# Feed-forward parts of a two-block model on one core: down products in four groups instead of three, and fixed places for split weights

## The chip, the cores and the metric

One NeuronCore of a Trainium2 chip runs one program. The metric is the device time of an execution in microseconds (us); less is better. Engines: TensorE (PE: matmuls, PEld: weight loads), VectorE (DVE), ScalarE (ACT), GpSimd (POOL), and SyncE (SP), whose queue issues the DMAs.

## The reference, cut to what matters

The model is two layers of a first block (feed-forward, mixer, feed-forward) and one second block (mixer, feed-forward). Five feed-forward parts have this form, on 528 tokens (512 and 16 meta tokens) or 512, with D_MODEL 1024 and D_FF 2816:

```python
def swiglu(x, w_gu, w_down):
    gate, up = jnp.split(x @ w_gu, 2, axis=-1)
    return (jax.nn.silu(gate) * up) @ w_down

h = h + 0.5 * swiglu(rms_norm(h, ffn_norm[l]), ffn_w_gu[l], ffn_w_down[l])
```

## The kernel before, in words

All activations are transposed: 8 tiles h[0..7] of 128 features by 528 (or 512) tokens stay on the chip. Every fp32 product is made of three matmuls in fp32r: weights and activations are split into a rounded part (hi) and the rest (lo), and PE adds hi·hi, hi·lo and lo·hi. Weights come from memory as *chunks* of 128 x 1024 fp32 or less into four raw tiles (RAW = 4, line 285); ACT copies the hi part (`hi`, line 364, tile whi) and DVE or POOL subtracts for the lo part (`lo`, line 367, tile wlo). A pair whi/wlo lies in one of five places (H = 5, line 284), taken in turn: chunk i goes to place i mod 5, and may be split only when chunk i-5 has been read.

A feed-forward part (`ffn`, line 559) has 22 tiles of 128 hidden features. In the five parts, called a0, b0, a1, b1 and c in order of time, gate and up of a plain tile are `gu(j)` (line 681): two chunks. All tiles of a0 are plain. In the other four only tiles 0 to 5 are; tiles 6 to 21 use a seven-product scheme: the gate and up chunk of a tile are added and subtracted in quarters on DVE, which gives four *parts* of weights (parts 0 to 2 with 1024 columns, part 3 with 512), and seven *products* (`product`, line 608) of 12 matmuls of 264 or 256 columns each. Tiles b11, B21, B22, T1 to T4 are the matching sums of activations. After the seventh product the hidden tile is split to gh and gl.

The down product of a group of hidden tiles is one chunk per output tile m (`d{group}.{m}`), accumulated over the group's tiles k in `down_steps` (line 728; one Item per k, three matmuls per column segment), then added to h[m] by DVE. THIRDS (line 29) makes three groups of 8, 7 and 7 tiles. The downs of groups 0 and 1 are interleaved by `weave` (line 267) with the products of the next group's tiles; those of group 2 come last, through `down` (line 705), without products beside them, and each finished h[m] goes to `nxt(m)`: `prep` (line 536) makes xh, xl and the sum of squares for the next stage, `prep_2` (line 1632) does so before the second block, `store` (line 2062) issues a DMA in part c.

The order of work around these stages is written out by `run` (line 329). The splitting steps of all chunks stand in one list in order of first use, and only its head can be issued. `between(cost)`, called after the matmuls of an Item and before its evacuation, issues as many steps as the cost has earned (0.9 per step, at most three saved up), while `allowed()` (line 425) holds for the head. Steps of a chunk that an Item needs are issued just before it at the latest. For Items marked `seven` (products and woven downs) the order of instructions on each engine is the order in which the code issues them (`InOrder`, line 239); chunks of such Items have their lo part on DVE, other chunks on DVE or, mostly, on POOL:

```python
e = nc.vector if i in sevens or i % 3 == 0 and c.split(".")[0] not in BUSY else nc.gpsimd
```

Of the kernel before, what the change touches and what calls it, by code (L numbers as in the profile page):

```python
# [8 lines left out]
F32 = mybir.dt.float32  # L9
# [17 lines left out]
NEG = -1e30  # L27
F_MIN = 1e-20
THIRDS = ((0, 8), (8, 15), (15, 22))
LEVELS = (64, 32, 16, 8, 4, 2)  # L30
TOPK = 128
TAKEN = -3e38
# [10 lines left out]
def chunk_table():  # L43

    table = {}

    def add(name, nk, m, make):
        table[name] = (len(table), nk, m, make)

    def cols(key, l, idx, r0=0, r1=None):  # L50
        return lambda a: _ktile(a[key][l][r0:r1][:, idx])

    def ffn(tag, l, gate, up, down):

        def gu(j):
            add(f"{tag}g{j}", KT, 128, cols(gate[0], l, np.arange(128) + gate[1] + 128 * j))
            add(f"{tag}u{j}", KT, 128, cols(up[0], l, np.arange(128) + up[1] + 128 * j))
        for j in range(NJ):
            gu(j)
        for t, (j0, j1) in enumerate(THIRDS):  # L60
            for m in range(KT):
                add(f"{tag}d{t}.{m}", j1 - j0, 128, cols(down, l, np.arange(128) + 128 * m, 128 * j0, 128 * j1))

    r = np.arange(128)
    for l in range(DEPTH):
        ffn(f"a{l}", l, ("ffn1_w_gu", 0), ("ffn1_w_gu", D_FF), "ffn1_w_down")
        for m in range(2):
            add(f"ckv{l}.{m}", KT, 128, cols("w_in", l, 384 + 128 * m + r))
        rot = np.arange(32)
        swap = np.concatenate([rot[16:], rot[:16]])  # L70
        add(f"kpe{l}", KT, 128, cols("w_in", l, 640 + np.concatenate([rot, rot, rot, swap])))
        for m in range(3):
            add(f"cq{l}.{m}", KT, 128, cols("w_in", l, 128 * m + r))
        for j in range(HG_HEADS):
            for i, n in enumerate("qfig"):
                add(f"h{n}{l}.{j}", KT, 128, cols("w_in", l, 672 + 512 * i + 128 * j + r))
        for m in range(KT):
            add(f"ga{l}.{m}", KT, 128, cols("w_in", l, 2720 + 128 * m + r))
            add(f"gb{l}.{m}", KT, 128, cols("w_in", l, 3744 + 128 * m + r))

        def v_cols(l=l):
            idx = (np.arange(MLA_HEADS)[:, None] * 128 + 64 + np.arange(64)[None]).reshape(-1)
            return cols("w_ukv", l, idx)
        add(f"v{l}", 2, 512, v_cols())

        def qk(j, l=l):
            q1 = np.concatenate([np.arange(64), 64 + rot, 64 + swap])
            parts = [cols("w_uq", l, (2 * j + i) * 96 + q1) for i in range(2)]
            k1 = np.concatenate([(2 * j + i) * 128 + np.arange(64) for i in range(2)])
            parts.append(cols("w_ukv", l, k1))  # L90
            return lambda a: np.concatenate([p(a) for p in parts], axis=1)
        for j in range(4):
            add(f"qk{l}.{j}", 8, 128, qk(j))

        def proj(m, l=l):
            pa, pb = cols("w_proj_attn", l, 128 * m + r), cols("w_proj_rec", l, 128 * m + r)
            return lambda a: np.concatenate([pa(a), pb(a)], axis=1)
        for m in range(KT):
            add(f"pj{l}.{m}", 8, 128, proj(m))
        for m in range(KT):  # L100
            add(f"wo{l}.{m}", KT, 128, cols("w_out", l, 128 * m + r))
        ffn(f"b{l}", l, ("ffn2_w_gu", 0), ("ffn2_w_gu", D_FF), "ffn2_w_down")

    def one(name, idx, m=128):
        add(name, KT, m, cols("w_in_2", 0, idx))
    r64 = np.arange(64)
    one("kk2", np.concatenate([1408 + r64, 1024 + r64]))
    for m in range(2):
        one(f"qi2.{m}", 1152 + 128 * m + r)
    one("vw2", np.concatenate([1088 + r64, 1472 + np.arange(4)]), 68)  # L110
    for m in range(4):
        one(f"u2.{m}", 128 * m + r)
    for m in range(4):
        one(f"q2.{m}", 512 + 128 * m + r)
    for m in range(KT):
        one(f"ga2.{m}", 1476 + 128 * m + r)
        one(f"gb2.{m}", 2500 + 128 * m + r)

    def two(key0, i0, key1, i1):
        p0, p1 = cols(key0, 0, i0), cols(key1, 0, i1)  # L120
        return lambda a: np.concatenate([p0(a), p1(a)], axis=1)
    for m in range(2):
        add(f"glu2.{m}", 8, 128, two("w_glu_2", 256 * m + r, "w_glu_2", 256 * m + 128 + r))
    for m in range(KT):
        add(f"pj2.{m}", 8, 128, two("w_proj_ssm_2", 128 * m + r, "w_proj_attn_2", 128 * m + r))
    for m in range(KT):
        add(f"wo2.{m}", KT, 128, cols("w_out_2", 0, 128 * m + r))
    ffn("c", 0, ("w_ffn_gate_2", 0), ("w_ffn_up_2", 0), "w_ffn_down_2")
    return table

# [73 lines left out]
class Scalar:  # L204


    def __init__(self, tc, e):
        self.tc, self.e, self.last = tc, e, None
# [27 lines left out]
        self.cost, self.fn, self.chunks, self.seven = cost, fn, tuple(chunks), seven  # L236


class InOrder:


# [40 lines left out]
class Kernel:  # L282
# [46 lines left out]
    def run(self):  # L329
# [12 lines left out]
        def load():  # L342
            nonlocal n_dma
            idx, nk, m, _ = CHUNKS[loads[n_dma]]
            t = self.wp.tile([128, 1024], F32, tag=f"raw{n_dma % self.RAW}", name=f"raw_{n_dma}")
            nc.sync.dma_start(t[:, :nk * m], self.ins["w"][idx, :, :nk * m])
            raws[loads[n_dma]] = t
            n_dma += 1

        def drop(c):  # L350
            raws.pop(c)
            gone[load_at[c]] = True
            while n_dma < len(loads) and (n_dma < self.RAW or gone[n_dma - self.RAW]):
                load()

        def hi_lo(i):
            if i not in made:
                made[i] = [self.wp.tile([128, 1024], F32R, tag=f"{x}{i % self.H}", name=f"w{x}_{i}") for x in ("hi", "lo")]
                n = 1024 if not isinstance(order[i], str) else CHUNKS[order[i]][1] * CHUNKS[order[i]][2]
                nk = 8 if not isinstance(order[i], str) else CHUNKS[order[i]][1]  # L360
                self.split_of[order[i]] = [t[:, :n].rearrange("p (k m) -> p k m", k=nk) for t in made[i]]
            return made[i]

        def hi(i, a, b, src):
            self.sc.activation(hi_lo(i)[0][:, a:b], src, AF.Copy)

        def lo(i, a, b, src, e=nc.vector):
            h, l = hi_lo(i)
            e.tensor_tensor(l[:, a:b], src, h[:, a:b].bitcast(F32), op=OP.subtract)

        def plus(out, a, b):
            nc.vector.tensor_tensor(out, a, b, op=OP.add)
# [42 lines left out]
        for it in self.prog:  # L415
            if it.seven:
                sevens.update(range(at, at + len(it.chunks)))
            at += len(it.chunks)
        queue = []
        for i in range(len(order)):  # L420
            queue += [x if isinstance(x, tuple) else (i, x) for x in steps_of(i)]
# [3 lines left out]
        def allowed():  # L425
            if n_step == len(queue):
                return False
            i = queue[n_step][0]
            return i < self.H or done[i - self.H]

        def step():
            nonlocal n_step
# [14 lines left out]

        self.between = between
        self.read = lambda c: done.__setitem__(index[c], True)
        load()  # L450
        self.setup(load)
        self.warm()
# [106 lines left out]
    def ffn(self, tag, n, st, alpha, nxt, gname=None, l=0):  # L559
# [167 lines left out]

        def down_steps(t, m):

            j0, j1 = THIRDS[t]  # L730
            nk = j1 - j0
            at = {}
            name = f"{tag}d{t}.{m}"

            def fn(k):
                if k == 0:
                    at["ps"] = self.accum(n)
                ps, cols = at["ps"]
                x = {k: g[j0 + k][0]}, {k: g[j0 + k][1]}
                self.mm3(ps, self.split_of[name], x, k, k, cols, k == 0, k == nk - 1)  # L740
                if k == nk - 1:
                    self.read(name)
                self.between(0.73)
                if k == nk - 1:
                    for q, (a, b) in zip(ps, cols):
                        hv = self.h[m][:, a:b]
                        nc.vector.scalar_tensor_tensor(hv, q, alpha, hv, op0=OP.mult, op1=OP.add)
                    if m == KT - 1:
                        for j in range(j0, j1):
                            self.free(*g.pop(j))  # L750
            return [Item(0.73, lambda k=k: fn(k), [name] if k == 0 else (), True) for k in range(nk)]

        c = 0.22 * 3
# [12 lines left out]
        if PLAIN_J < NJ:  # L766
            for j in range(PLAIN_J):
                add_gu(j)
            for j in range(PLAIN_J, THIRDS[0][1]):
                self.prog += products(j)  # L770
            for t in (0, 1):
                p = [x for j in range(*THIRDS[t + 1]) for x in products(j)]
                self.prog += p[:4] + weave(p[4:-4], [x for m in range(KT) for x in down_steps(t, m)]) + p[-4:]
            add_down(2)
            return
        for j in range(0, 9):
            add_gu(j)
# [1306 lines left out]
```

## Time and profile before

| | |
|---|---|
| median of 3 runs | 3183.62 us (3178.26 to 3184.14) |
| profiled execution, its own time | 3182.51 us |
| span of its trace | 3180.7 us |
| PE busy | 3118.5 us, 98% |
| DVE busy | 2072.9 us, 65% |
| ACT busy | 1377.7 us, 43% |
| POOL busy | 852.9 us, 27% |

The span runs from the first to the last instruction; the execution's own time is 1.8 us longer. Matmuls are pipelined: a matmul is shown busy for longer than the next one waits, so busy time says less than the spacing of starts. "Idle before" is time in which an engine had nothing to run, with the engine and tile that ended it. A row of a view by stretches gives the stretch, its length, the busy time of PE, PEld, DVE, ACT and POOL (or of one engine) with the number of instructions in brackets, the granted TensorE clock as a share of 2.4 GHz, the DMA engines' busy share and GB/s.

### The profile page before, as it was taken

What the parts mean: (1) busy time and instruction counts of PE and PEld (TensorE: products, weight loads), DVE (VectorE), ACT (ScalarE), POOL (GpSimd) and SP (SyncE); (2) the same over time, 40 slices, a digit from 0 to 9 for tenths busy, and PEclk for the clock granted to TensorE, in tenths of its full rate; (3) what the DMA queues carried; (4) which work ended last, traced back from release to release, by engine and by line L of the source; (5) the groups of instructions that cost most, each with busy time, mean ns of one, the idle gap of its engine ahead of it and who ended that gap; (6) DMA issues with size and microseconds to landing.
All of it is one profiled execution on the core that took longest, in us unless ns stands there. A gap on an engine that the chain in (4) does not pass through costs nothing. (4 is left out here: it accounts for less than half of the span.)

```text
span 3180.7 us, 52625 instructions
## 1 busy us (share of the span) xinstructions
PE 3118.5 (98%) x21530; PEld 2872.4 (90%) x21530; DVE 2072.9 (65%) x3552; ACT 1377.7 (43%) x2355; POOL 852.9 (27%) x493
## 2 busy tenths in 40 slices
PE   9999999999999999999999999999999999999999
PEld 9999999899999999999998888888998777888888
DVE  7664466763676666866666674577667587577674
ACT  5322345544344434444444553444346435444442
POOL 3553235543220002100034453330003543230001
PEclk9999999999999999999999999999999999999999
DMA  6333331111222233223332112222334432222332
GB/s 199 123 99 108 94 94 56 44 58 61 93 80 93 88 99 113 67 94 97 94 109 74 41 47 74 86 93 74 105 107 152 124 101 73 67 93 73 99 103 91
DMA packets 106530, 289.61 MB, mean 91 GB/s; under 512 B 23088, under 2 KB 32304, under 8 KB 106288
## 3 DMA queue, kind: packets, MB, share of 16 engines
q1 hardware_dynamic: 106288, 286.24, 28.5%
q8 instruction: 169, 2.77, 0.4%
q14 instruction: 73, 0.60, 0.1%
HBM read 272.96 MB, written 13.24 MB: 90 GB/s over the span
## 5 line engine op out<-in xcount | busy, mean ns | idle before, releaser
L249 POOL TENSOR_TENSOR wlo<-raw,whi 128x1024 fp32r<-128x1024 f32 (+1 forms) x217 | 541.2, 2496 | 1965.2 <-ACT whi L249 1668.3
L249 ACT ACTIVATE whi<-raw 128x1024 fp32r<-128x1024 f32 (+2 forms) x632 | 537.9, 866 | 817.2 <-PE bank L249 417.3
L249 PE MATMUL bank<-xh,whi 128*128 128x264 f32 (+1 forms) x2504 | 811.8, 325 | 4.8 <-DVE t L249 4.3
L249 PE MATMUL bank<-xl,whi 128*128 128x264 f32 (+1 forms) x2504 | 811.3, 324 | 5.0 <-DVE xl L249 4.9
L249 PE MATMUL bank<-xh,wlo 128*128 128x264 f32 (+1 forms) x2504 | 804.9, 322 | 1.3 <-POOL wlo L249 1.3
L249 PEld LDWEIGHTS bank<-xl,whi 128*128 128x128 f32 x2504 | 476.1, 190 | 34.9 <-DVE xl L249 6.8
L249 PEld LDWEIGHTS bank<-xh,whi 128*128 128x128 f32 x2504 | 475.2, 190 | 35.4 <-issue 4.7
L249 PEld LDWEIGHTS bank<-xh,wlo 128*128 128x128 f32 x2504 | 475.6, 190 | 27.1 <-issue 1.7
L249 PE MATMUL bank<-gh,wlo 128*128 128x264 f32 (+1 forms) x1408 | 440.6, 313 | 12.1 <-DVE wlo L249 12.1
L249 DVE TENSOR_TENSOR wlo<-raw,whi 128x1024 fp32r<-128x1024 f32 (+2 forms) x351 | 368.5, 1052 | 123.0 <-ACT whi L249 120.2
L249 PE MATMUL bank<-gh,whi 128*128 128x264 f32 (+1 forms) x1408 | 439.7, 312 | 0.0
L249 PE MATMUL bank<-gl,whi 128*128 128x264 f32 (+1 forms) x1408 | 439.5, 312 | 0.0
L249 PEld LDWEIGHTS bank<-gh,wlo 128*128 128x128 f32 x1408 | 265.1, 188 | 30.2 <-DVE wlo L249 14.6
L249 PEld LDWEIGHTS bank<-gh,whi 128*128 128x128 f32 x1408 | 265.2, 188 | 8.4 <-issue 0.4
L249 PEld LDWEIGHTS bank<-gl,whi 128*128 128x128 f32 x1408 | 265.2, 188 | 8.3
L249 ACT ACTIVATE p<-p,nm 128x144 f32<-128x144 f32 (+8 forms) x104 | 57.0, 548 | 224.5 <-DVE nm L249 217.0
L249 PE MATMUL bank<-T2h,whi 128*128 128x264 f32 (+1 forms) x512 | 146.5, 286 | 3.8 <-DVE c L249 3.5
L249 DVE SCALAR_TENSOR_TENSOR h<-bank,h 128x264 f32<-128x264 f32 (+1 forms) x192 | 88.7, 493 | 92.2 <-PE bank L249 91.2
L249 PE MATMUL bank<-T2h,wlo 128*128 128x264 f32 (+1 forms) x512 | 145.8, 285 | 1.8 <-DVE wlo L249 1.8
L249 PE MATMUL bank<-B21h,whi 128*128 128x264 f32 (+1 forms) x512 | 145.5, 284 | 0.9 <-ACT zu L249 0.9
L249 PE MATMUL bank<-B21h,wlo 128*128 128x264 f32 (+1 forms) x512 | 145.3, 284 | 0.0
L249 PE MATMUL bank<-B21l,whi 128*128 128x264 f32 (+1 forms) x512 | 145.0, 283 | 0.0
(373 smaller groups left out, 6641.9 us busy)
## 6 DMA issues: line engine op xcount, KB each, us to landing
raw<-in_w_dram SPq DMA_DIRECT2D x423, 512.0 KB, 3.5
raw<-in_w_dram SPq DMA_DIRECT2D x80, 448.0 KB, 3.3
h<-in_x_dram SPq DMA_DIRECT2D x8, 264.0 KB, 6.9
s_t<-zero SPq DMA_DIRECT2D x8, 256.0 KB, 3.5
s_wo<-cm SPq DMA_DIRECT2D x16, 128.0 KB, 3.2
s_win<-cm SPq DMA_DIRECT2D x8, 256.0 KB, 2.0
s<-s_win SPq DMA_DIRECT2D x8, 256.0 KB, 4.2
s<-s_wo SPq DMA_DIRECT2D x8, 256.0 KB, 4.1
```

The source lines that it names most:

```text
L249: i = f(*args, **kw)
```

## The change

The four parts with seven-product tiles get GROUPS of 6, 6, 5 and 5 tiles; a0 keeps THIRDS. The downs of groups 0, 1 and 2 are woven with the products of groups 1, 2 and 3; in the first weave no product leads (before, 14 products of tiles 6 and 7 and four more stood ahead of it). The downs of group 3 are Items of the `seven` kind too, and call `nxt`. The places: within such a phase, part r has the place r of the five (counted from the one after the last plain chunk), downs alternate between place 4 ("even") and the second half of place 3 plus a small tile `rest` ("odd"), and a step waits for the last user of its own place only. The list of steps stays one list.

```diff
+GROUPS = ((0, 6), (6, 12), (12, 17), (17, 22))
...
+class Pieces:
+    def __getitem__(self, at):
+        p, k, m = at
+        return self.a[p, k, m] if k < self.n else self.b[p, k - self.n, m]
...
         def hi_lo(i):
             if i not in made:
-                made[i] = [self.wp.tile([128, 1024], F32R, tag=f"{x}{i % self.H}", name=f"w{x}_{i}") for x in ("hi", "lo")]
...
+                tag, phase, what = place[i]
+                if phase is None:
+                    t = pair(tag, i)
+                else:
+                    if (phase, tag) not in phases:
+                        phases[phase, tag] = pair(tag, f"p{phase}_{tag}")
+                    t = phases[phase, tag]
+                n, nk = cols_of(i)
+                if what != "odd":
+                    made[i] = [[(0, x)] for x in t]
...
+                else:
+                    made[i] = [[(0, x[:, 512:]), (512, self.rest[:, 256 * h:256 * h + 256])] for h, x in enumerate(t)]
...
         def hi(i, a, b, src):
-            self.sc.activation(hi_lo(i)[0][:, a:b], src, AF.Copy)
+            for c, e, x, _ in pieces(i, a, b):
+                self.sc.activation(x, src[:, c:e], AF.Copy)
...
+        place, need, users, phases = [], [], {}, {}
+        c, phase, downs = 0, 0, 0
+        for i in range(len(order)):
+            if i not in sevens:
+                if i and i - 1 in sevens:
+                    c += 5
+                tag = c % self.H
+                c += 1
+                place.append((tag, None, "all"))
+                need.append(list(users.get(tag, {}).values()))
+                users[tag] = {"all": i}
+                continue
+            if i - 1 not in sevens:
+                phase, downs = phase + 1, 0
+            if isinstance(order[i], str):
+                r, what = (4, "even") if downs % 2 == 0 else (3, "odd")
+                downs += 1
+            else:
+                r, what = order[i][0], "part"
+            tag = (c + r) % self.H
+            place.append((tag, phase, what))
+            u = users.get(tag, {})
+            if "all" in u:
+                u = users[tag] = {"was": u["all"]}
+            need.append([u[what]] if what in u else [u["was"]] if "was" in u else [])
+            u[what] = i
...
-            i = queue[n_step][0]
-            return i < self.H or done[i - self.H]
+            return all(done[i] for i in need[queue[n_step][0]])
...
+        self.rest = self.wp.tile([128, 512], F32R, tag="rest", name="rest")
...
+                    if t == len(GROUPS) - 1:
+                        nxt(m)
...
-            for j in range(PLAIN_J, THIRDS[0][1]):
-                self.prog += products(j)
-            for t in (0, 1):
-                p = [x for j in range(*THIRDS[t + 1]) for x in products(j)]
-                self.prog += p[:4] + weave(p[4:-4], [x for m in range(KT) for x in down_steps(t, m)]) + p[-4:]
-            add_down(2)
+            for t in range(len(GROUPS) - 1):
+                p = [x for j in range(*GROUPS[t + 1]) for x in products(j)]
+                lead = 4 if t else 0
+                self.prog += p[:lead] + weave(p[lead:-4], [x for m in range(KT) for x in down_steps(t, m)]) + p[-4:]
+            d = [down_steps(len(GROUPS) - 1, m) for m in range(KT)]
+            self.prog += d[0][:-1] + d[1][:-1] + d[0][-1:] + d[1][-1:] + [x for y in d[2:] for x in y]
             return
```

## Rows read from the trace of the kernel before

**Rows 1.** The page, busy time, share of the span, instructions of an engine.

```profile
PE 3118.5 (98%) x21530; PEld 2872.4 (90%) x21530; DVE 2072.9 (65%) x3552; ACT 1377.7 (43%) x2355; POOL 852.9 (27%) x493
```

**Rows 2.** By stretches: parts b0, a1, b1, c after tile 5; then single stages.

```profile
966.20:1265.50 299.30, 294.63 (x2401) 292.82 (x2400) 202.70 (x331) 131.82 (x230) 18.64 (x8) 1.00 0.32 99
1337.20:1638.80 301.60, 296.90 (x2401) 294.89 (x2401) 200.48 (x331) 131.55 (x230) 18.20 (x9) 0.99 0.32 100
2168.60:2457.90 289.30, 284.64 (x1872) 258.24 (x1871) 201.98 (x309) 140.00 (x244) 25.56 (x14) 1.00 0.35 110
2887.60:3176.60 289.00, 284.49 (x1872) 258.46 (x1871) 183.48 (x292) 117.02 (x211) 11.13 (x5) 1.00 0.30 96
...
966.20:992.70 26.50, 26.50 (x218) 26.37 (x217) 24.18 (x42) 16.31 (x31) 0.00 (x0) 1.00 0.31 101
2418.80:2457.90 39.10, 39.10 (x170) 31.48 (x169) 31.62 (x30) 28.05 (x40) 21.60 (x13) 1.00 0.58 193
3137.60:3176.60 39.00, 39.00 (x170) 31.50 (x169) 12.79 (x12) 5.05 (x6) 8.47 (x4) 1.00 0.25 90
2891.10:2905.10 14.00, 14.00 (x120) 14.00 (x119) 13.01 (x23) 7.49 (x16) 0.00 (x0) 1.00 0.37 115
```

**Rows 3.** Waits of PE in part b0: us in total, times, longest.

```profile
PE bank L249 <- DVE wlo L249: 3.8, 4, 1.8
PE bank L249 <- DVE c L249: 0.9, 1, 0.9
```

**Rows 4.** Timeline of DVE and ACT behind tile 5, part c; last b0.

```profile
2887.88 0.69 DVE L249 TENSOR_TENSOR t<-bank,R 128x512 f32<-128x512 f32 x1 [4.60 <-PE bank L249]
2888.61 0.69 DVE L249 TENSOR_TENSOR t<-t,s 128x512 f32<-128x512 f32 x1
2889.33 0.63 ACT L249 ACTIVATE gh<-t 128x512 fp32r<-128x512 f32 x1 [5.33 <-DVE t L249]
2889.87 0.62 ACT L249 ACTIVATE whi<-raw 128x512 fp32r<-128x512 f32 x1
...
968.27 0.62 ACT L249 ACTIVATE whi<-raw 128x512 fp32r<-128x512 f32 x1
```

**Rows 5.** Groups by form, DVE and ACT: busy us, mean ns, idle before.

```profile
L249 DVE TENSOR_TENSOR wlo<-raw,whi 128x1024 fp32r<-128x1024 f32 x176 | 226.3, 1286 | 75.2 <-ACT whi L249 73.8 <-ACT pt L249 0.3
L249 DVE TENSOR_TENSOR wlo<-raw,whi 128x512 fp32r<-128x512 f32 x128 | 88.2, 689 | 41.5 <-ACT whi L249 40.2
...
L249 DVE TENSOR_TENSOR wlo<-raw,whi 128x896 fp32r<-128x896 f32 x47 | 54.7, 1165 | 6.4 <-ACT whi L249 6.1
...
L249 ACT ACTIVATE whi<-raw 128x512 fp32r<-128x512 f32 x256 | 152.1, 624 | 141.0 <-PE bank L249 80.6 <-issue 41.3 <-DVE raw L249 17.5
L249 ACT ACTIVATE whi<-raw 128x896 fp32r<-128x896 f32 x80 | 75.0, 946 | 118.9 <-PE bank L249 54.0 <-issue 36.8 <-DMA raw<-in_w_dram 13.2
```

**Rows 6.** Timeline of one `prep_2`, end of b1; last one `prep`, end of b0.

```profile
2444.10 0.68 DVE L249 SCALAR_TENSOR_TENSOR h<-bank,h 128x512 f32<-128x512 f32 x1
2444.82 0.63 ACT L249 ACTIVATE sq<-h 128x512 f32<-128x512 f32 x1 [0.27 <-DVE h L249]
2446.78 0.71 ACT L249 ACTIVATE xh<-h,gains 128x512 fp32r<-128x512 f32 x1
2448.16 0.74 DVE L249 SCALAR_TENSOR_TENSOR xl<-h,gains,xh 128x512 fp32r<-128x512 f32 x1
...
1252.75 0.76 DVE L249 SCALAR_TENSOR_TENSOR xl<-h,gains,xh 128x528 fp32r<-128x528 f32 x1
```

**Rows 7.** By stretches, PE alone: the 8 us behind a stall; one stall.

```profile
1023.40:1031.40 8.00, 8.00 (x65) 1.00 0.60 199
2698.40:2706.40 8.00, 8.00 (x38) 0.79 0.20 66
...
2698.40 0.66 PE L249 MATMUL bank<-ident,p 128*128 128x128 f32 x4 [3.04 <-ACT p L249]
```

**Rows 8.** DMA issues: KB each, median us to landing.

```profile
raw<-in_w_dram SPq DMA_DIRECT2D x423, 512.0 KB, 3.5
```

More of the change, by code (lines that the diff above doesn't have):

```diff
@@ L51, in cols, with ffn @@
         return lambda a: _ktile(a[key][l][r0:r1][:, idx])
-    def ffn(tag, l, gate, up, down):
+    def ffn(tag, l, gate, up, down, groups=GROUPS):
         def gu(j):
@@ L59, in ffn @@
             gu(j)
-        for t, (j0, j1) in enumerate(THIRDS):
+        for t, (j0, j1) in enumerate(groups):
             for m in range(KT):
@@ L65, in chunk_table @@
     for l in range(DEPTH):
-        ffn(f"a{l}", l, ("ffn1_w_gu", 0), ("ffn1_w_gu", D_FF), "ffn1_w_down")
+        ffn(f"a{l}", l, ("ffn1_w_gu", 0), ("ffn1_w_gu", D_FF), "ffn1_w_down", GROUPS if l else THIRDS)
         for m in range(2):
@@ L236, in __init__ @@
         self.cost, self.fn, self.chunks, self.seven = cost, fn, tuple(chunks), seven
+class Pieces:
+    def __init__(self, a, n, b):
+        self.a, self.n, self.b = a, n, b
+    def __getitem__(self, at):
+        p, k, m = at
+        return self.a[p, k, m] if k < self.n else self.b[p, k - self.n, m]
 class InOrder:
@@ L354, in drop, with cols_of, pair @@
                 load()
+        def cols_of(i):
+            return (1024, 8) if not isinstance(order[i], str) else (CHUNKS[order[i]][1] * CHUNKS[order[i]][2], CHUNKS[order[i]][1])
+        def pair(tag, name):
+            return [self.wp.tile([128, 1024], F32R, tag=f"{x}{tag}", name=f"w{x}_{name}") for x in ("hi", "lo")]
         def hi_lo(i):
             if i not in made:
-                made[i] = [self.wp.tile([128, 1024], F32R, tag=f"{x}{i % self.H}", name=f"w{x}_{i}") for x in ("hi", "lo")]
@@ L359, in hi_lo @@
-                n = 1024 if not isinstance(order[i], str) else CHUNKS[order[i]][1] * CHUNKS[order[i]][2]
-                nk = 8 if not isinstance(order[i], str) else CHUNKS[order[i]][1]
-                self.split_of[order[i]] = [t[:, :n].rearrange("p (k m) -> p k m", k=nk) for t in made[i]]
-            return made[i]
+                tag, phase, what = place[i]
[5 more added lines that the diff above has]
+                    t = phases[phase, tag]
@@ new lines, in hi_lo @@
+                n, nk = cols_of(i)
+                if what != "odd":
+                    made[i] = [[(0, x)] for x in t]
+                    self.split_of[order[i]] = [x[:, :n].rearrange("p (k m) -> p k m", k=nk) for x in t]
+                else:
+                    made[i] = [[(0, x[:, 512:]), (512, self.rest[:, 256 * h:256 * h + 256])] for h, x in enumerate(t)]
+                    self.split_of[order[i]] = [Pieces(x[:, 512:].rearrange("p (k m) -> p k m", k=4), 4,
+                                                      self.rest[:, 256 * h:256 * h + n - 512].rearrange("p (k m) -> p k m", k=nk - 4))
+                                               for h, x in enumerate(t)]
@@ L364, in hi, with pieces @@
+            return made[i]
+        def pieces(i, a, b):
+            h, l = hi_lo(i)
+            for n, ((c, x), (_, y)) in enumerate(zip(h, l)):
+                e = min(b, h[n + 1][0] if n + 1 < len(h) else b)
+                if e > max(a, c):
+                    yield max(a, c) - a, e - a, x[:, max(a, c) - c:e - c], y[:, max(a, c) - c:e - c]
         def hi(i, a, b, src):
-            self.sc.activation(hi_lo(i)[0][:, a:b], src, AF.Copy)
+            for c, e, x, _ in pieces(i, a, b):
+                self.sc.activation(x, src[:, c:e], AF.Copy)
@@ L367, in lo @@
         def lo(i, a, b, src, e=nc.vector):
-            h, l = hi_lo(i)
-            e.tensor_tensor(l[:, a:b], src, h[:, a:b].bitcast(F32), op=OP.subtract)
+            for c, d, x, y in pieces(i, a, b):
+                e.tensor_tensor(y, src[:, c:d], x.bitcast(F32), op=OP.subtract)
         def plus(out, a, b):
@@ L728, in down_steps @@
         def down_steps(t, m):
-            j0, j1 = THIRDS[t]
+            j0, j1 = GROUPS[t]
             nk = j1 - j0
```

## The prediction

> **What bounds the kernel now.** I read the page first, then the four changed parts by stretches, then what PE waited for in them, then the timelines at their two edges. PE is busy for 98% of the span and nothing else comes near [rows 1], so the change can win only where PE stands still or repeats work. It removes no matmul: a part has 16 x 7 x 12 = 1344 matmuls of products and 22 x 8 x 3 = 528 of downs (1056 of 264 columns on 528 tokens), before and after.
>
> What is there to win follows from the spacing. On 528 tokens, 216 matmuls of products take 26.5 us, 0.1227 each; on 512, 119 take 14.0 us, 0.1176 each, and 168 downs 39.0 us, 0.2321 each [rows 2]. So b0 and a1 would need 2400 x 0.1227 = 294.5 us behind tile 5, and b1 and c 1344 x 0.1176 + 528 x 0.2321 = 280.6 us. They take 299.3, 301.6, 289.3 and 289.0: 4.8, 7.1, 8.7 and 8.4 us more, 29 together. The idle time of PE in the same rows is 4.7 + 4.7 + 4.7 + 4.5 = 18.5 us [rows 2]; each wait costs a little more than its idle time, since PE starts up again. I take 25 us as the ceiling. In b0 the idle time is four waits for split downs or parts and one for an evacuation [rows 3]; the other three parts show the same.
>
> In the program's order the place of these waits is plain. The five places are shared in turn, so beside long downs the list gets no further than one or two chunks ahead, and twice in a part (third down of each weave) the split is issued just before its use. DVE is nearly full only where products run without downs (24.2 of 26.5 us); in the last downs it has room (31.6 of 39.1 and 12.8 of 39.0) [rows 2].
>
> **The change, part by part.** *Separate places.* With its own place each down can be split while the one before it is read, and each part while other parts are read. In the new order, read from the code, the list stays two to five chunks ahead in all three weaves, so the waits of [rows 3] go. But two pairs of weaves now meet, not one, and at each 8 products run without downs, where the evacuation wait (0.9 us) stood [rows 3]: two such waits and small ones stay, 1.5 us a part, 6 in all. Gain 25 - 6 = 19 us, at most 25, at least 10.
>
> *Eight more evacuations of h a part.* One costs 0.68 us on DVE [rows 6]; over b0 DVE is busy for 202.7 of 299.3 us [rows 2], so they are hidden. DMA moves the same bytes.
>
> *Start of the phase.* This is what I expect to decide. The first item is now down 0, k = 0. Its place is "even", r = 4 counted from the one after the last plain chunk: that is the place of tile 5's up chunk. So its split can't be issued before tile 5 is through, and since only the head of the list can be issued, the parts of tile 6, whose places are free, stand behind it. Before, three parts were split during tiles 4 and 5. Now the row of work on the in-order engines is, in part c [rows 4]: PE is through at 2887.6; DVE scales t (2887.88), multiplies (2888.61), ACT copies gh (2889.33), and only then, at 2889.87, the next copy on ACT, which becomes the hi part of the down. It has 768 columns, between 0.624 and 0.946 us [rows 5], 0.84: PE starts at 2890.7, 3.1 us late. The lo part (between 0.689 and 1.165 us [rows 5], 1.0) ends at 2891.7, and the third matmul waits for it: 0.5 more. Then come, first needed and first issued, the two sums of part 0 (like a lo of 512 columns, 0.69, spaced 0.6) and its lo of 1024 (1.29 [rows 5]): 2894.1. PE wants it at 2892.3: 1.8 more. With three restarts of 0.17: 5.9 us. In b0 the copy slot is at 968.27 [rows 4] against 966.2: 2.9 + 0.6 + 1.4 + 0.5 = 5.4. Two of each: 22.6 us.
>
> A stall of this length also costs clock. Nine stalls of PE with 1.9 us or more of idle time stand in this trace, and behind all nine the granted clock fell to its lower level (1.2 GHz) for a time; one row stands: 0.79 on average over the next 8 us, so 0.21 x 8 = 1.7 us lost [rows 7]. Behind the shorter stall of 1.8 us in b0 it stayed at 1.00 [rows 3, 7]; a1, with 0.99 over the whole part, lost some [rows 2]. Here PE would be waiting for DVE during much of that time, so I take half: 0.8 a part, 3 in all. The start costs 26 us; bounds: 12 if only the first stall shows, 30 with the full clock loss.
>
> The Trainium skill ("TensorE: Matmul & The Clock Gate", Part 1) says that low speed is the default state and activity releases it. By that rule every start stall would pay a slow stretch too, the upper bound of 30 us; the trace agrees for stalls like these, at 0.79.
>
> *Last downs.* A group of 5 gives PE 15 matmuls a chunk, 15 x 0.2321 = 3.5 us (3.7 on 528 tokens), where it had 4.9. Two places serve them, so chunk m+2 can be split only once chunk m is read, and all of it is now in program order, lo on DVE (before, mostly on POOL, five chunks deep). In that order `nxt(0)`, split hi of chunk 3, `nxt(1)`, lo of chunk 3 follow each other. Hi of chunk 2 has only the last step of chunk 1 (0.7 us) as cover: 0.2 + 0.5 us with restarts 0.9, in every part. For c that is all, since `store` issues only DMAs.
>
> In b0 and a1 the lo of chunk 3 stands behind h (0.7), xh (0.72), xl (0.76 [rows 6]) of m = 0 and the same with the sum (0.7) of m = 1: about 7.6 us after chunk 0 is read; PE wants it at 5.65. 2.1 with restart, so 3.1 a part, and 0.5 more in a1, where the mixer needs the last xl at once. After that a chunk needs 3.0 us of DVE and 0.7 of waiting for xh, which 3.7 us of PE just cover.
>
> In b1 a chunk needs far more: from the end of h to the end of xh are 2.7 us on ACT (2444.78 to 2447.49 [rows 6]), and the hi of a later chunk stands behind that. Two of these chains put hi of chunk 3 at 5.6 and its lo at 10.6 us, against 4.9 and 6.3 on PE: 0.9 + 4.5; one cycle of hi (0.7), lo (0.8), h (0.7) and chain (2.7) is 4.9 us against PE's 3.5, so later chunks run up again, 0.5 at chunk 7; and the last xh comes some 9 us after PE's last down, where the second block's first product has 5 us of other work: 4. With chunk 2's 0.9 and two clock losses of 1.7 (half of them counted): 13. Together 3.1 + 3.6 + 13 + 0.9 = 21; bounds 4 (only chunk 2's) and 32 (both clock losses, drift in b0 and a1 too).
>
> **Sum.** From the profiled execution, 3182.5 us: -19 + 26 + 21 = +28, so 3210.5; it stands 1.1 us below the median of the runs, so 3211.6, rounded to 3211.
>
> **Rivals.**
> *A, the places pay and the edges are free: faster.* The same waits at the same steps in all four parts speak for it, and the full 19 to 25 us would give 3159 to 3165. Against it: the first down's place is the one PE read last, which no order of engines can hide. It decides for faster if start and end together stay below 19 us, so the start at about 3 a part with the end at 4. The Trainium skill ("Perfetto Trace Analysis", Optimization Strategy) says that a gap repeating on the engine that should be full can mean too few buffers, and that regimes with different limits are worth interleaving; by this rule the sum would be A's. The trace agrees that the gaps repeat; it doesn't show the edges.
> *B, only the start costs.* If next-stage work in the last downs is hidden as it is now (DVE 31.6 of 39.1 us [rows 2]), 3183.6 - 19 + 26 + 4 = 3195. Against it: PE's cover per chunk falls by 1.4 us while ACT and DVE's work per chunk stays.
> *C, the order doesn't bind at the edges.* If hi and lo of the first down ran ahead of gh's chain, only 1.9 us would be left at each start: 3183.6 - 19 + 8 + 4 = 3177, and with 21 at the end 3194. Against it: the split behind gh stands right behind gh in [rows 4].
> *D, raw loads become late.* With two downs to a tile in the second and third weave, the second raw tile of a pair is freed some 4.4 us of PE work before its first use, and landing takes 3.5 [rows 8]. One us at each of 8 tiles in four parts would add 30: 3242.
>
> **How the numbers follow.** Chances: the forecast 0.60, B 0.15, A 0.10, C 0.08, D 0.07. What a measurement of this kernel can tell from no change is 0.2%, 6.4 us. Faster by more: A and a quarter of C, 0.12. Within: the rest of A's and C's near cases and the low end of B, 0.09. Slower: 0.79. For the range I leave out A and C's low end and half of D: from 3188 (start 20, end 5) to 3232 (gain 10, start 28, end 29). The likeliest case's own range is 3200 to 3225.
>
> **What would show it.** Right: PE idle for about 3 us before the first down behind tile 5, then for a wlo of the down and one of part 0, at four places; the clock below 1 behind them; no wait for wlo at the third down of a weave; in b1's last downs idle of 4 us before chunk 3, waiting for DVE, and a longer wait for xh before the second block. Wrong: a whi of the first down that ends before gh, or no idle in the last downs (B), or raw tiles as releasers in the weaves (D).

## The result and the profile after

The changed kernel takes 3235.39 us (median of four runs, 3231.86 to 3238.20), the kernel before 3180.94 beside it: a ratio of 1.0178 [1.0166, 1.0190], some 57 us more. I had forecast +28 and a range up to 3232. The sign and the two places named as costs were right; the size was about half.

The page, first part, and the four parts behind tile 5 by stretches (columns as in [rows 2], which hold the same stretches of before):

```profile
PE 3133.2 (97%) x21530; PEld 2882.1 (89%) x21530; DVE 2106.4 (65%) x3717; ACT 1395.8 (43%) x2451; POOL 810.5 (25%) x472
...
967.20:1274.80 307.60, 297.66 (x2400) 295.57 (x2400) 210.38 (x382) 137.89 (x259) 4.83 (x2) 0.99 0.30 96
1346.00:1653.70 307.70, 297.48 (x2402) 295.33 (x2401) 210.34 (x381) 137.30 (x258) 3.48 (x3) 0.99 0.30 95
2192.30:2495.00 302.70, 289.14 (x1872) 261.60 (x1872) 208.22 (x352) 141.82 (x268) 4.50 (x5) 0.98 0.31 102
2934.40:3228.60 294.20, 286.42 (x1873) 259.79 (x1872) 198.25 (x338) 124.56 (x241) 0.00 (x0) 0.99 0.30 97
```

Same matmuls, and each part longer than in [rows 2]: by 8.3, 6.1, 13.4 and 5.2 us, 33 together. Of the span's 52 us more, 18.5 lie behind the parts: from the end of a1 to the start of b1 538.6 us where there were 529.8, from the end of b1 to the start of c 439.4 where there were 429.7.

What PE waited for in part b0 (answers to [rows 3]):

```profile
PE bank L261 <- DVE wlo_p L261: 3.9, 4, 1.8
PE bank L261 <- ACT zu L261: 3.1, 3, 1.8
PE bank L261 <- ACT whi_p L261: 2.8, 1, 2.8
```

The old waits (wlo, c) are gone, others stand in their place. The single stalls say where. First the start, in the timelines of PE, ACT and DVE behind tile 5 of b0 (ACT's second row answers to the last of [rows 4]):

```profile
967.03 0.28 PE L261 MATMUL bank<-xh,wlo 128*128 128x264 f32 x1
970.09 0.39 PE L261 MATMUL bank<-gh,whi_p 128*128 128x264 f32 x1 [2.78 <-ACT whi_p L261]
971.09 0.39 PE L261 MATMUL bank<-gh,wlo_p 128*128 128x264 f32 x1 [0.48 <-DVE wlo_p L261]
973.42 0.59 PE L261 MATMUL bank<-b11h,wlo_p 128*128 128x264 f32 x1 [1.29 <-DVE wlo_p L261]
...
968.67 0.64 ACT L261 ACTIVATE gh<-t 128x528 fp32r<-128x528 f32 x1 [5.99 <-DVE t L261]
969.22 1.87 ACT L261 ACTIVATE whi_p<-raw 128x768 fp32r<-128x768 f32 x3
...
970.07 0.96 DVE L261 TENSOR_TENSOR wlo_p<-raw,whi_p 128x768 fp32r<-128x768 f32 x1
```

The rows show the forecast chain: gh, behind it the hi part of down 0, then its lo part, then part 0. The extra spacing is 2.9, 0.6 and 1.5 us (forecast 2.9, 0.6 and 1.4 before restarts); the other three parts show the same chain (in c 3.03 and 1.12 idle, against 3.1 and 1.8, and no wait for the lo part of down 0, forecast at 0.5).

Second the clock behind it: PE alone in the 16 us behind the end of tile 5, in the four parts (columns as in [rows 7]):

```profile
967.10:983.10 16.00, 11.45 (x70) 0.79 0.23 72
1346.00:1362.00 16.00, 11.46 (x70) 0.79 0.26 73
2192.30:2208.30 16.00, 11.11 (x57) 0.79 0.23 72
2934.30:2950.30 16.00, 11.72 (x62) 0.79 0.27 86
```

The granted clock is 0.79 over 16 us, double the time of the row in [rows 7], so much of it was at the lower level (1.2 GHz). In 16 us shortly before the end of tile 5 PE was busy throughout, at a granted clock of 1.00, in all four parts.

Third, a wait that the sum had put at nothing: DVE, ACT and PE in the first weave of b0.

```profile
1017.29 0.69 DVE L261 TENSOR_TENSOR s<-raw 128x512 f32<-128x512 f32 x1 [4.39 <-DMA raw<-in_w_dram]
1018.50 1.22 DVE L261 TENSOR_TENSOR wlo_p<-raw,whi_p 128x1024 fp32r<-128x1024 f32 x1
1019.98 0.68 DVE L261 TENSOR_TENSOR raw<-s,raw 128x512 f32<-128x512 f32 x1
...
1020.74 0.63 ACT L261 ACTIVATE whi_p<-raw 128x512 fp32r<-128x512 f32 x1 [5.04 <-DVE raw L261]
1021.80 0.37 ACT L261 ACTIVATE zu<-bank 128x264 f32<-128x264 f32 x1
...
1022.22 0.39 PE L261 MATMUL bank<-B21h,whi_p 128*128 128x264 f32 x1 [1.07 <-ACT zu L261]
```

DVE stands for 4.39 us for a weight load; its sums, and ACT's copies of them, come late; behind these on ACT stands the evacuation zu, for which PE waits. It comes mostly at tiles 9 and 11 of a part. Over the whole span:

```profile
PE bank L261 <- ACT zu L261: 13.4, 12, 2.2
```

Fourth the last downs. In b1 the lo of chunk 3 came as forecast (answer to the term for [rows 6]); PE's timeline:

```profile
2471.24 0.50 PE L261 MATMUL bank<-gh,whi_p 128*128 128x512 f32 x1 [0.52 <-ACT whi_p L261]
2476.19 0.80 PE L261 MATMUL bank<-gh,wlo_p 128*128 128x512 f32 x1 [4.21 <-DVE wlo_p L261]
```

At the end of a1, PE, DVE and POOL show more than forecast:

```profile
1663.64 0.59 PE L261 MATMUL bank<-xh,whi 128*128 128x264 f32 x1 [6.99 <-ACT xh L261]
...
1654.00 2.09 DVE L261 SCALAR_TENSOR_TENSOR xl<-h,gains,xh 128x528 fp32r<-128x528 f32 x1 [0.81 <-ACT xh L261]
1656.01 2.85 DVE L261 TENSOR_TENSOR sq<-sq,sq 128x528 f32<-128x528 f32 x1
1658.78 3.35 DVE L261 TENSOR_TENSOR wlo<-raw,whi 128x1024 fp32r<-128x1024 f32 x1
1662.06 0.76 DVE L261 SCALAR_TENSOR_TENSOR h<-bank,h 128x264 f32<-128x264 f32 x2
1663.62 0.77 DVE L261 SCALAR_TENSOR_TENSOR xl<-h,gains,xh 128x528 fp32r<-128x528 f32 x1 [0.80 <-ACT xh L261]
1664.31 0.70 DVE L261 TENSOR_TENSOR sq<-sq,sq 128x528 f32<-128x528 f32 x1
...
1653.12 7.94 POOL L261 TENSOR_TENSOR wlo<-raw,whi 128x1024 fp32r<-128x1024 f32 x3
```

PE is through with the last downs at 1653.7, but h[7] is made only at 1662.06: in front of it on DVE stands a split of the next stage, and it and two steps of m = 6 (xl and sq) ran two to four times as long as elsewhere, beside three such splits on POOL. I had put 0.5 us here.

### The profile page after: what moved, and what is told of

Read it like the earlier page. It is cut to its first block, busy times and chain, and to the rows that moved or that the text cites. A ratio compares the mean times of both kernels' runs of the same rounds, so it can differ in the third digit from the quotient of the medians.

```text
span 3232.7 us, 53061 instructions
## 1 busy us (share of the span) xinstructions
PE 3133.2 (97%) x21530; PEld 2882.1 (89%) x21530; DVE 2106.4 (65%) x3717; ACT 1395.8 (43%) x2451; POOL 810.5 (25%) x472
## 5 line engine op out<-in xcount | busy, mean ns | idle before, releaser
L261 ACT ACTIVATE whi<-raw 128x1024 fp32r<-128x1024 f32 (+1 forms) x280 | 291.7, 1047 | 545.8 <-PE bank L261 309.3
L261 DVE TENSOR_TENSOR wlo_p<-raw,whi_p 128x512 fp32r<-128x512 f32 (+3 forms) x320 | 266.9, 834 | 138.3 <-ACT whi_p L261 127.5
L261 ACT ACTIVATE whi_p<-raw 128x512 fp32r<-128x512 f32 (+2 forms) x384 | 245.5, 652 | 255.5 <-DVE raw L261 110.6
L261 PE MATMUL bank<-gh,whi_p 128*128 128x264 f32 (+1 forms) x912 | 295.6, 324 | 12.2 <-ACT whi_p L261 12.1
L261 PE MATMUL bank<-gh,wlo_p 128*128 128x264 f32 (+1 forms) x912 | 296.2, 325 | 10.1 <-DVE wlo_p L261 9.8
L261 PE MATMUL bank<-gl,whi_p 128*128 128x264 f32 (+1 forms) x912 | 294.8, 323 | 0.0
L261 PEld LDWEIGHTS bank<-gh,wlo_p 128*128 128x128 f32 x912 | 172.9, 190 | 27.4 <-DVE wlo_p L261 13.7
L261 PEld LDWEIGHTS bank<-gh,whi_p 128*128 128x128 f32 x912 | 172.8, 189 | 21.1 <-ACT whi_p L261 15.1
L261 PEld LDWEIGHTS bank<-gl,whi_p 128*128 128x128 f32 x912 | 172.9, 190 | 6.3
L261 PE MATMUL bank<-B21h,whi_p 128*128 128x264 f32 (+1 forms) x512 | 147.4, 288 | 13.9 <-ACT zu L261 13.4
```

What stands on the lines that cost most here:

```text
L261: i = f(*args, **kw)
```

## The experiments

Theory: three separate costs, at the start of the phase (the place of down 0), in the first weave (raw tiles reused in ring order) and in the last downs (two places with the next stage's work in program order), over a gain from separate places. Effects below are differences of ratios to the kernel before, times 3181 us; 0.1% is 3.2 us.

**1. Down 0 gets the place that is free at the start.** The places of the phase are shifted by one.

```diff
-                r, what = (4, "even") if downs % 2 == 0 else (3, "odd")
+                r, what = (0, "even") if downs % 2 == 0 else (4, "odd")
...
-                r, what = order[i][0], "part"
+                r, what = order[i][0] + 1, "part"
```

> The order of work stays as in the changed kernel; only the places are counted from another start, so that the first down and parts 0 and 1 of tile 6 fall on places that are free during the last plain tile. Theory (the down's place is the one PE read last, and one list holds the parts back): the three stalls behind tile 5 (2.9 to 3.2, 0.4 to 0.65, 1.4 to 1.75 us) go in all four parts, and with them the slow clock behind them, some 8 us a part: 3235 - 32 = 3203, granted clock about 0.99. Rival 1 (the added DVE work sets the time, wherever the stall shows): under 8 us less, 3227 or more. Rival 2 (the cause is that downs come first in the order, not their place): no change, 3235.

Measured 3198.85 us, 1.0067 [1.0051, 1.0084]: 35 us less than the change. PE alone, the same 16 us behind tile 5, b0 and b1:

```profile
963.90:979.90 16.00, 16.00 (x133) 1.00 0.34 107
...
2178.60:2194.60 16.00, 16.00 (x111) 1.00 0.35 113
```

The start stalls are gone and the clock stays at its upper level. In the same 16 us the change started 70, 70, 57 and 62 matmuls where this kernel starts 133, 134, 111 and 111, so it lost 7.6, 7.6, 7.8 and 7.1 us (16 x (1 - 70/133) and so on), 30 in all. Some 18 of them are idle time; the other 12, 3 a part, are clock and restarts. The remaining 5 us are inside the intervals of the two ratios; at the parts' ends PE's waits for xh fell from 7.9 to 5.5 us and for xl from 7.8 to 4.6, which may be part of them. The waits for zu stay (14.2 us).

**2. Four products lead in the first weave too, as before.**

```diff
-                lead = 4 if t else 0
+                lead = 4
```

> Four products lead the first weave again; places as in the changed kernel. Theory: the stalls behind tile 5 go (-32), but two raw loads of the first weave (second raw tile of tiles 8 and 11) are now freed only 0.7 us of PE work before their first use, so that PE's waits for the ACT copy zu in the first weave grow from some 3.5 to 6 or 7 us a part (+13): about 3216. Rival 1 (DVE work): 3227 or more, waits for zu unchanged. Rival 2 (order, not place): 3203, waits for zu unchanged.

Measured 3201.92, 1.0075 [1.0058, 1.0092]: 33 us less. The start stalls go in this way too: they came from the first item and the place together. My expectation that later loads would take back a part failed; the waits for zu fell to half:

```profile
PE bank L261 <- ACT zu L261: 7.3, 9, 1.8
```

So the few us of lead that I read from the order of the code did not tell here what a late load costs.

**3. Raw tiles from a list of free ones instead of in ring order.** A load may take any raw tile that has been read.

```diff
+        raw_free, slot = list(range(self.RAW)), {}
...
+            slot[loads[n_dma]] = raw_free.pop(0)
...
-            while n_dma < len(loads) and (n_dma < self.RAW or gone[n_dma - self.RAW]):
+            raw_free.append(slot[c])
+            while n_dma < len(loads) and raw_free:
```

> Raw tiles are taken from a list of free ones instead of in turn; four of them, as before, and all else as in the changed kernel. Theory (PE's waits for zu come from raw loads that are issued 2 to 3 us of PE work before use, because the ring makes them wait for the tile just split): every load is now issued at least 4.3 us of PE work ahead; PE's waits for zu fall from 13.4 us to under 3, the stalls behind tile 5 and in the last downs stay: 3235 - 13 = 3222. Rival 1 (DVE work, or the split pieces on ACT): waits for zu and time as they are, 3235.

Measured 3218.31, 1.0124 [1.0109, 1.0139]: 17 us less. PE's waits over the span:

```profile
PE bank L261 <- DVE wlo_p L261: 15.7, 13, 4.2
PE bank L261 <- ACT whi_p L261: 12.1, 5, 3.0
...
PE bank L261 <- ACT zu L261: 0.9, 4, 0.2
```

The waits for zu are nearly gone (13.4 us in the change), while those of the start and the end are what they were (15.1 and 12.1 in the change). Late loads are a cost of their own, and the steps stand in the same list as before, so it was the loads and not the list that held the weaves up.

The same list in the kernel before:

> The kernel before with the list of free raw tiles alone. Theory: there the shortest raw load of the weaves is issued 3.7 us of PE work ahead, against some 3.5 us to landing, so next to nothing is late: 3178, at most 3 less. Rival (raw loads hold up every version alike): 10 or more less, as in the changed kernel.

Measured 3177.61, 1.0002 [0.9993, 1.0011]: no difference. The ring of raw tiles cost nothing in the order of before; it was the change's order that made loads late.

**4. The last group in the plain order of before.** Not `seven` Items: the next stage's preparation and splits are ordered by their due times again.

```diff
+        G = GROUPS if PLAIN_J < NJ else THIRDS
...
-                if t == 2:
+                if t == len(G) - 1:
...
-            d = [down_steps(len(GROUPS) - 1, m) for m in range(KT)]
-            self.prog += d[0][:-1] + d[1][:-1] + d[0][-1:] + d[1][-1:] + [x for y in d[2:] for x in y]
+            add_down(len(GROUPS) - 1)
```

> The downs of the last group go through the plain path again (five places, lo part mostly on POOL, order left to the framework), all else as in the changed kernel. Theory (two places and the written order put the split behind the preparation of the next stage): waits for split downs in the last group go, and the waits for xh and xl behind a1 and b1 (7.2 and 6.8 us) fall back to 3 and under 1: 2.5 + 8 + 13 us less, 3211; stalls behind tile 5 and in the weaves stay. Rival 1 (DVE work): a gain as well, since POOL takes two thirds of the lo parts (some 18 us off DVE), but it would show as shorter waits in the weaves too. Rival 3 (a group of 5 is too short to cover a split on any path): the waits in the last group stay, 3230.

Measured 3212.00, 1.0106 [1.0090, 1.0121]: 23 us less. The waits over the span that were 15.1, 7.9 and 7.8 us in the change:

```profile
PE bank L261 <- DVE xl L261: 8.1, 8, 2.0
...
PE bank L261 <- DVE wlo_p L261: 4.7, 6, 1.2
...
PE bank L261 <- ACT xh L261: 2.1, 2, 1.5
```

The waits for lo parts and the 7 us wait for xh go, the longest for xl falls from 4.6 to 2.0. PE's waits for zu rise meanwhile, from 13.4 to 18.0 us. This kernel changes the order and, with it, the number of places (five) and who makes the lo parts, so it doesn't say which of the three counts.

**5. Written order kept, five places for the last group.** Downs 2, 3, 4 and 7 of the last group take places of the parts.

```diff
+                if last[0] == "3" and last[1] not in "0156":
+                    r, what = {"2": 0, "3": 1, "4": 2, "7": 0}[last[1]], "part"
...
```

> The changed kernel; the last group's down products keep their written-out order, but take five places of the split activations in turn (three of the down products and both of the pairs), so that a place is reused only five down products later. Theory (two different costs in the tail: down products that share two places, and the written-out order, which lets splits of the next stage go ahead of the last activation): the waits for split down products of the last group go (some 2 us each in the parts of the first layer, 5 in the first of the second layer, with their clock some 12 in all), and the waits behind the parts for the next stage's rows (7 and 6 us) stay: 3223 us. Rival 1, the places are the whole cause of the tail's cost: 3212, as with the plain tail. Rival 2, the order alone costs: no change, 3235.

Measured 3228.16, 1.0151 [1.0133, 1.0169]: 9 us less where 12 were expected (the two intervals allow some 7 us either way), but not in the way that I had given:

```profile
PE bank L261 <- ACT whi L261: 20.0, 4, 13.1
...
PE bank L261 <- DVE wlo_p L261: 5.4, 7, 1.3
PE bank L261 <- POOL wlo L261: 5.3, 4, 1.8
...
PE bank L261 <- ACT xh L261: 1.5, 1, 1.5
```

The waits for split downs go, as the theory said. But those for the next stage's rows no longer show either, since a longer one covers them: PE now waits for the next stage's weights (whi, 13.1 us behind b1, 3.3 behind b0 and a1). Behind b1 ACT makes that split at 2490.68, behind the xh of seven of the eight rows. By the order of the code that is because the downs hold all five places to the end; no run tests it alone. With the order written out, few places delayed the downs here and many delayed the next stage.

**6. Groups alone:** the kernel before with groups of 6, 6, 5, 5, its places shared in turn, four leading products and its plain last group.

```diff
-            for t in (0, 1):
-                p = [x for j in range(*THIRDS[t + 1]) for x in products(j)]
+            for t in range(len(GROUPS) - 1):
+                p = [x for j in range(*GROUPS[t + 1]) for x in products(j)]
...
-            add_down(2)
+            add_down(len(GROUPS) - 1)
```

> The kernel before with groups of 6, 6, 5, 5 alone: five shared places in turn, four products ahead of every weave, plain path for the last group. Theory: shorter downs alone let the list stay two or three chunks ahead, so the waits for split downs in the weaves (3 to 4 us a part) go, but four raw loads a part are issued 2.2 us of PE work before use and bring 1.5 to 2 us each of waits for zu: about the kernel before, 3182, between 3172 and 3190. Rival (the places are what the weaves need): the waits for split downs come at every one of the three weaves, 3200.

Measured 3175.57, 0.9995 [0.9986, 1.0004]: no difference either way. The waits for wlo (13.8 us before) are gone here too, without separate places, but waits for evacuations where products run alone take their place (3.5 us in four waits before):

```profile
PE bank L250 <- DVE c L250: 9.1, 12, 1.1
```

**7. The repairs 1, 3 and 4 together.**

> The changed kernel with the three edits together: first down and parts on free places, raw tiles from a list of free ones, last group through the plain path. Theory: the three costs are separate waits and add up: 36 + 17 + 23 = 76 us less than 3235, 3159, under the kernel before (3178) by some 0.6%. Rival 1 (DVE has no room for what is then left): the gains overlap, 3175 or more.

Measured 3164.81, 0.9962 [0.9949, 0.9974], faster than before. The single repairs sum to 75 us and together give 69, the same within the intervals. The parts now take 293.3, 293.2, 282.7 and 283.0 us, 27 less than in [rows 2], with DVE as busy as before (205.4 us in b0, against 202.7), so its added work is not what made the change slow. But the stretch behind b1 is 7.8 us longer than before. With lead 4 as well:

> As the kernel with the three edits, with four products ahead of the first weave too. Theory: with free places and early loads it no longer matters which comes first: within 4 us of that kernel, about 3160. Rival (the unmixed products are what costs): 5 to 10 us more.

Measured 3165.14, 0.9962 [0.9949, 0.9976]: the same. With places free and loads early, the order of the first items made no difference.

**8. Groups of 6, 5, 5, 6 on top of it,** so that the last downs have more work (group 1 has less).

```diff
-GROUPS = ((0, 6), (6, 12), (12, 17), (17, 22))
+GROUPS = ((0, 6), (6, 11), (11, 16), (16, 22))
```

> The three repairs together (down products start in the other place, raw tiles from a free list, last group in plain order), with groups of 6, 5, 5, 6 instead of 6, 6, 5, 5 tiles. Theory (what is left over the gain is the end of a part, where a last group of 5 tiles, 0.6 of a group's work less than 6, gives the next stage's preparation less cover: 6 us of waits behind the first part of the second layer, 2 to 3 behind the others): a last group of 6 halves these, 3161 us. Rival, the ends wait for the length of the preparation's own chain, not for cover: the same as with 6, 6, 5, 5, 3165 us.

Measured 3154.55, 0.9919 [0.9906, 0.9933], the best of all, 26 us under before. The span is 10.6 us shorter than in experiment 7 (3152.4 against 3163.0), where 4 were expected. PE's waits behind b1, first with 6, 6, 5, 5:

```profile
PE bank L261 <- DVE xl L261: 3.9, 2, 2.0
...
PE bank L261 <- ACT xh L261: 1.5, 1, 1.5
```

and with 6, 5, 5, 6:

```profile
PE bank L261 <- ACT xh L261: 0.8, 1, 0.8
PE bank L261 <- DVE xl L261: 0.6, 1, 0.6
```

Four us less. The rest of what this stretch gained goes with the clock. The 16 us behind b1, PE alone, with 6, 6, 5, 5:

```profile
2438.30:2454.30 16.00, 10.59 (x31) 0.79 0.78 251
```

and with 6, 5, 5, 6:

```profile
2435.40:2451.40 16.00, 14.62 (x59) 1.00 0.86 276
```

Behind three waits of 1.5 to 2.0 us in a row the granted clock was 0.79, behind two of 0.8 and 0.6 it stayed at 1.00. The whole stretch from b1 to c is 6.9 us shorter (430.6 against 437.5), of 10.6 in the span.

**9. The same without separate places:** groups of 6, 5, 5, 6, free list, plain last group, five places in turn.

```diff
+GROUPS = ((0, 6), (6, 11), (11, 16), (16, 22))
...
+            while n_dma < len(loads) and raw_free:
```

> The kernel before with groups of 6, 5, 5, 6 tiles, every pair of weaves mixed, raw tiles from a free list, the last group in plain order, four products ahead of each weave, and the five places shared in turn as before: so the best kernel so far without the separate places. Theory (with the clock undisturbed the separate places are worth what their absence left in the kernel with 6, 6, 5, 5 and shared places, 9 us of waits for evacuations and the parts' ends): 3165 us, some 10 above the kernel with separate places. Rival 1, places are worth nothing once the groups are right: 3155. Rival 2, shared places with short groups lose more, by the waits for evacuations and their clock: 3175, no better than with 6, 6, 5, 5 and shared places.

Measured 3163.81, 0.9956 [0.9943, 0.9970], as the theory said. That is 9 us above experiment 8 by the medians and 12 by the ratios, and PE's waits name it: they are for c, and the kernel of experiment 8 has none of these.

```profile
PE bank L250 <- DVE c L250: 8.9, 10, 1.1
```

So the separate places do pay, some 10 us, by letting the products without downs run free of evacuation waits, not by the waits for split weights (wlo) of [rows 3], which the shorter groups remove anyway. The two kernels differ in two more things: the lead of the first weave, which made no difference in experiment 7, and the small tile `rest`, whose share no run separates.

## Why the prediction missed its size

In ratios, the change is +57 us: -12 (experiment 7 against before) + 35 (start) + 17 (loads) + 23 (end) - 6 (overlap of the three, within the intervals). The forecast was -19 + 26 + 21, and nothing for loads.

**The step that failed** is "the list stays two to five chunks ahead in all three weaves, so the waits of [rows 3] go", with 1.5 us a part left for all weaves. Those waits did go, and the list of splits was far enough ahead; the loads in front of it weren't, a term that the sum put at nothing. I had this mechanism as rival D and gave it 0.07, looking in the second and third weave, where two downs go with a tile, and for one us at each of eight tiles. It struck in the first weave, at two tiles of a part, with 13.4 us of waits; experiment 3 took 17 us back. The raw tiles should have been followed one by one, as the places were.

**Mis-sized: the clock at the start.** "I take half: 0.8 a part, 3 in all." With the restarts (2 us of the 22.6) that made 5; clock and restarts measured 12, about 3 a part. The stalls themselves, 20.6 without restarts, were 18.3 us of idle time. Taking half was wrong, and so was the row: in b0 the clock was as low in the second 8 us (0.77) as in the first (0.80), while [rows 7] lost as much only in one stretch of 8 us. Two of the nine stalls of before had lost as much as these four starts (last section), so the trace that I read held the higher price too. The Trainium skill's rule cited there (low speed is the default state, "TensorE: Matmul & The Clock Gate", Part 1) spoke for the upper bound; the trace agrees, at 0.79 in all four parts, and the start's 30 us, as experiment 1 measures it, reached it.

**The last downs** were forecast at 21 and measured 23, but that the sum came out is luck, since the shares were others: 0.5 in a1's end became the longest wait there (6.99), from work of the next stage ahead of h[7] on DVE, while c and the first splits cost less than forecast. What I called the cause, too few places with all of it in program order, is not settled: with more places alone (experiment 5) the wait moved to the next stage's weights and 9 of the 23 us came back.

**The gain** of 19 was 12 with 6, 6, 5, 5. In the parts of the profiled executions it was there (27 us), more than the ceiling of 25: the evacuation waits that I had kept, 1.5 us a part, don't come, and b0's 293.3 us lie under the 294.5 that I took as its least. But 2.8 us were given back behind a1 and 7.8 behind b1, where a last group of 5 tiles doesn't cover `prep_2`. Experiment 8 keeps it: 26 us over the whole kernel. Two of the range's sums are off by one to two us: 3183.6 - 19 + 20 + 5 is 3189.6, not 3188, and 3183.6 - 10 + 28 + 29 is 3230.6, not 3232.

**The rivals.** A's condition, edges free, was what experiments 7 and 8 made. In ratios they are 12 and 26 us under the kernel before, where A had said 19 to 25. The Trainium skill's rule beside A ("Perfetto Trace Analysis", Optimization Strategy: a repeating gap can mean too few buffers) is half borne out: the repeating gap went with shorter groups alone (experiment 6), and buffers paid some 10 us at another gap (experiment 9). B is ruled out by the stalls in the last downs and C by those at the start, in the section on the result.

Left open: why experiment 2 halved the waits for zu instead of lengthening them, and how much of experiment 4 is the order, how much the five places and how much the lo parts on POOL.

## What to carry to other kernels

When buffers are separated but the steps that fill them are still issued from one in-order list, look at the head of the list at both ends of the phase: one step whose buffer is read last holds up all that have theirs free (30 to 35 us here). Follow every resource in the chain, the load tiles as well as the split tiles, through the new order; a ring that never waited before may wait now. And leave enough work in the last group to cover the next stage's preparation: one tile more there was worth some 10 us.

## What the runs showed of the hardware

Splits on POOL slow work on DVE. Beside three splits on POOL (7.94 us), xl, sq and a lo of 1024 columns took 2.09, 2.85 and 3.35 us on DVE; xl and sq took 0.77 and 0.70 a few us later in the same rows, and such a lo 1.22 elsewhere. The Trainium skill ("SBUF — State Buffer", "SBUF: two separate sides") says that the pair of ports which the two engines share is locked for a whole instruction; the trace agrees, with three slow operations beside three on POOL.

Stalls of like length can cost different amounts of clock. The kernel before, PE alone, in the 16 us behind two single stalls (3.18 and 2.42 us of idle time):

```profile
1732.45:1748.45 16.00, 16.00 (x94) 0.79 0.21 67
1852.42:1868.42 16.00, 16.00 (x106) 0.89 0.21 67
```

PE was busy throughout behind both, and the first lost twice as much. Of the nine stalls that the prediction counts, seven are like the second (0.79 over 8 us, as in [rows 7]) and two like the first (0.79 over 16 us; the other had 3.48 us of idle time, at 2600.18). The change's four starts, with 2.78, 0.48 and 1.29 us of idle time in b0, are all like the first. Whether the second and third stall kept the clock down there isn't shown, since no stall followed the one at 1732.45.
